# A two-block model on one core: attention masks on full rows, gate sigmoids at eviction, two modulation products moved, expert selection tied to the weight splits

## The chip, the core and the metric

One NeuronCore of a Trainium2 chip: TensorE (PE) for matmuls, VectorE (DVE), ScalarE (ACT), GpSimd (POOL) and the DMA queue of SyncE (SP). The metric is the device time of one execution in microseconds; a kernel is given by the median of its runs.

## The reference, cut to what matters

Two transformer-like blocks of width 1024 over 256 tokens, in float32. Block one mixes an mLSTM with four heads and an attention with eight heads of 64, gates the two with sigmoids, and ends in a gated feed-forward layer. With 256 tokens and blocks of 256 keys the attention is plain causal attention.

```python
mod = jnp.dot(c_act, ada_w[l]) + ada_b[l]
sh1, sc1, g1, sh2, sc2, g2 = jnp.split(mod, N_MOD, axis=-1)
h = modulate(rms_norm(x, norm1_g[l]), sh1, sc1)
z = jnp.einsum('bsd,de->bse', h, w_in[l]) + b_in[l]
...
ym = (hm.reshape(B, S, M_WIDTH) * jax.nn.sigmoid(mo)).astype(x.dtype)
ya = merge_heads(moba_attention(qa, ka, va))
merged = (jax.nn.sigmoid(ga) * jnp.einsum('bsm,md->bsd', ym, p_mlstm[l])
          + jax.nn.sigmoid(gb) * jnp.einsum('bsa,ad->bsd', ya, p_moba[l]))
x = x + g1[:, None, :] * jnp.einsum('bsd,de->bse', merged, w_out[l])
```

Block two has a pooling and a state-space mixer (SSD) with 16 heads and then chooses, for each token and each of eight heads, 16 of 16384 experts by product keys:

```python
seg = a_cs[..., :, None] - a_cs[..., None, :]
decay = jnp.exp(jnp.where(causal, seg, -jnp.inf))
...
v1, i1 = lax.top_k(s1, PEER_TOPK)
v2, i2 = lax.top_k(s2, PEER_TOPK)
top_s, pos = lax.top_k(cand, PEER_TOPK)
gates = jax.nn.softmax(top_s, axis=-1)
```

All 16384 experts are computed for all tokens as dense matmuls, and the gates choose among them afterwards.

## The kernel before

All weights stream through TensorE as slabs of 128 x 1024 (512 KB). A slab is loaded by SP (`raw`), copied by ScalarE into the rounded format fp32r (`hi`, L213), and the rest `lo = raw - hi` is formed by VectorE (L218) or GpSimd (L216). The activations are split in the same way, and each product is three matmuls (`mm3`, L273 to L276): 24 matmuls of 256 columns for a slab in `proj`. The order of the slabs is written out in the list `items` (L158 to L192); the modulation products ("ada", kind "d") lie between them: each loads 512 KB and is one VectorE multiplication with a sum (L230). `prep` works two slabs ahead (`LA = 2`); `hi` and `lo` have three buffers each, and a projection ends in one of three PSUM buffers `pp`. Other matmuls write to five buffers `sp`.

`cur["gp"]` says that every gp-th split goes to GpSimd; it is 2 from the eighth query slab to the 28th expert slab and otherwise 0. Side work is written as generators: `tick()` after a projection runs one step of the first one in `gens`.

The code states an order, and a planner in the framework chooses the final order on each engine by its own model of the times. `after(ins, prev)` (L89) fixes that `ins` stands behind `prev`; `act` fixes an activation behind its table load, and `table` a table load behind all activations of the table before.

Block one: the mLSTM (generator `mlstm`, L552), rotation of the query and key slabs (`rope`), value slabs, then 16 gate slabs (L717 to L722) whose results are evicted by ScalarE with a bias (L721), with `moba` (L659), the attention, as the generator beside them. `moba` makes the scores (L671, L672) in four groups of two banks: 128 queries against 256 keys, then 128 against 128; a mask of -1e30 is added by a matmul with an identity. After the 16 slabs come the sigmoid table, the mLSTM's output gate, one sigmoid over all of `sg`, and the merge (`pmo`, eight slabs, L740 to L751), then `wout`.

Block two: the decay masks of the 16 SSD heads (L926 to L933), made by a 48-row matmul and two mask matmuls for each head. The expert selection is the generator `topk` (L1083), four times: (head half, token half), about 16 steps each, beside 8 of the 16 query slabs and the 64 first expert slabs (`dblock`). The 64 next ones have `gstage` beside them, which builds the gate matrix.

Of the kernel before, what the change touches and what calls it, by code (L numbers as in the profile page):

```python
# [61 lines left out]
def two_block_kernel(ctx, tc, I, out, dbg=None):  # L62
# [120 lines left out]
    w_items("win", 28, ada_list(1, [2, 3, 4], "d"), 2)  # L183
    w_items("pmo", 8)
# [108 lines left out]
    gens = []  # L293

# [91 lines left out]
    with p1:  # L386
# [330 lines left out]
        for ab in range(2):  # L717
            for i in range(8):
                ps = pp()
                proj(ps)  # L720
                S.activation(sg[:, i, ab], ps[:, :T], AF.Identity, bias=pc("bga" if ab == 0 else "bgb", i))  # L721
                tick()  # L722
# [6 lines left out]
        for h in range(4):  # L729
            V.scalar_tensor_tensor(hm[:, h], hm[:, h], pc("mng", h), smo[:, h], OP.mult, OP.mult)  # L730
            S.activation(ymH[:, h], hm[:, h], AF.Copy)
            V.tensor_tensor(ymL[:, h], hm[:, h], ymH[:, h].bitcast(F32), OP.subtract)
        act(sg, sg, AF.Sigmoid)
# [99 lines left out]
    with ExitStack() as p3:  # L833
# [52 lines left out]
        identb = q3.tile([P, P], BF, name="identb")  # L886
        V.tensor_copy(identb, ident)
        trib = q3.tile([P, P], BF, name="trib")
        V.tensor_copy(trib, cs_("mB"))
# [32 lines left out]
        for i in (8, 9, 10, 11):  # L922
# [3 lines left out]
            for h in range(4 * i - 32, 4 * i - 28):  # L926
                ab = sp()
                se = id16[:, h:h + 1].to_broadcast([48, P])
# [145 lines left out]
    with ExitStack() as p4:  # L1074
# [8 lines left out]
        def topk(hq, tt):  # L1083
# [3 lines left out]
            for hf in range(2):  # L1087
# [8 lines left out]
                for h in range(4):  # L1096
                    V.max(v[:, h, 0:8], s_[:, h])
                    V.max_index(x[:, h, 0:8], v[:, h, 0:8], s_[:, h])
                    V.match_replace(s_[:, h], v[:, h, 0:8], s_[:, h], -3.0e38)
                    V.max(v[:, h, 8:16], s_[:, h])  # L1100
                    V.max_index(x[:, h, 8:16], v[:, h, 8:16], s_[:, h])
                    yield
# [5 lines left out]
            V.tensor_tensor(cand, vv[0].unsqueeze(3).to_broadcast([P, 4, 16, 16]),  # L1108
                            vv[1][:, :, None, :].to_broadcast([P, 4, 16, 16]), OP.add)
# [3 lines left out]
            for h in range(4):  # L1113
                ch = cand[:, h].rearrange("p a b -> p (a b)")
                V.max(ts_[:, h, 0:8], ch)
# [45 lines left out]
        for i in range(16):  # L1161
# [313 lines left out]
```

## Time and profile before

| | |
|---|---|
| median of the runs | 1427.33 us (1427.19 to 1429.57) |
| the profiled execution | 1433.29 us, span 1431.5 us |
| TensorE busy | 1389.7 us, 97% |
| VectorE busy | 1155.1 us, 81% |
| ScalarE busy | 708.8 us, 50% |
| GpSimd busy | 61.3 us, 4% |
| chain that ended last | PE 85%, DVE 10%, ACT 2%, DMA 2% |
| DMA | 285.92 MB, mean 200 GB/s |

A busy TensorE in the profile is one with a matmul in flight; since matmuls overlap, the count of matmuls in a stretch says more about its pace than its busy time. The granted clock is given as a share of 2.4 GHz. Two engines that stand for each other show up as idle time with the name of the instruction that ended it.

### The profile page before, as it was taken

The numbers are of one execution on the slowest core, as the hardware profiler recorded it, in microseconds if no ns is written. First come the engines' busy times: TensorE is split into PE (matmuls) and PEld (weight loads), VectorE is DVE, ScalarE is ACT, GpSimd is POOL, SyncE is SP. The second block draws the span as 40 slices with busy tenths as digits, with TensorE's granted clock in tenths as the row PEclk, the third lists the DMA queues.
The fourth block names the chain that finished last, engine by engine and source line by source line (L and its number), as shares of the span: only waits on it lengthen the run. The fifth ranks groups of instructions, "written<-read, shape, count | busy, mean of one in ns | idle before, by whom it ended". The sixth has DMA issues, their size and how long they took to land.

```text
span 1431.5 us, 28913 instructions
## 1 busy us (share of the span) xinstructions
PE 1389.7 (97%) x11842; PEld 1341.2 (94%) x11842; DVE 1155.1 (81%) x1995; ACT 708.8 (50%) x1052; POOL 61.3 (4%) x50
## 2 busy tenths in 40 slices
PE   8999989999999999998899999999999999999997
PEld 6888779899999788998899999999999999999997
DVE  7999558988888597789956978989689999675554
ACT  4555465554546846555554544444444443444443
POOL 0000000000000000123420000000000000000001
PEclk9999889999999999999999999999999999999999
DMA  9988416699995353554455555555655555676663
GB/s 319 341 289 314 148 47 192 229 350 343 330 317 207 104 155 125 163 161 149 162 188 181 177 166 174 163 165 172 180 164 161 177 161 172 200 215 213 208 205 103
DMA packets 78921, 285.92 MB, mean 200 GB/s; under 512 B 8786, under 2 KB 9186, under 8 KB 78660
## 3 DMA queue, kind: packets, MB, share of 16 engines
q1 hardware_dynamic: 78484, 282.60, 60.6%
q8 instruction: 93, 1.52, 0.4%
q0 software_dynamic: 304, 1.47, 0.3%
q14 instruction: 40, 0.33, 0.1%
HBM read 282.99 MB, written 1.05 MB: 198 GB/s over the span
## 4 chain that ended last, share of the span: by engine, by line
PE 85%; DVE 10%; ACT 2%; DMA 2%; issue 1%; SPq 0%; DVEq 0%; ACTq 0%
PE pp L274 17%; PE pp L276 17%; PE pp L275 17%; PE sp L1271 9%; PE sp L1274 8%; PE sp L1275 8%; DVE lo L218 3%; PE pp L1210 2%; ACT hi L213 1%; PE sp L671 1%; DMA raw<-in_wst 0%; DVE raw L230 0%; DMA ada<-in_wst 0%; DVE M L965 0%; PE sp L929 0%
## 5 line engine op out<-in xcount | busy, mean ns | idle before, releaser
L213 ACT ACTIVATE hi<-raw 128x1024 fp32r<-128x1024 f32 x382 | 404.6, 1060 | 562.7 <-PE pp L275 282.9
L218 DVE TENSOR_TENSOR lo<-raw,hi 128x1024 fp32r<-128x1024 f32 x364 | 450.3, 1238 | 141.3 <-ACT hi L213 140.5
L276 PE MATMUL pp<-nH,lo 128*128 128x256 f32 x1064 | 301.6, 285 | 16.1 <-DVE lo L218 16.1
L274 PE MATMUL pp<-nH,hi 128*128 128x256 f32 x1064 | 300.0, 283 | 1.5 <-ACT fs L107 0.9
L275 PE MATMUL pp<-nL,hi 128*128 128x256 f32 x1064 | 300.3, 283 | 0.0
L1271 PE MATMUL sp<-wHL,hi 128*128 128x256 f32 x992 | 279.5, 283 | 0.0
L1274 PE MATMUL sp<-wHL,hi 128*128 128x256 f32 x992 | 277.7, 281 | 0.0
L1275 PE MATMUL sp<-wHL,lo 128*128 128x256 f32 x992 | 273.8, 281 | 0.0
L274 PE MATMUL pp<-hH,hi 128*128 128x256 f32 (+1 forms) x824 | 237.0, 288 | 1.3 <-ACT sg L721 1.3
L276 PE MATMUL pp<-hH,lo 128*128 128x256 f32 (+1 forms) x824 | 234.6, 285 | 0.0
L275 PE MATMUL pp<-hL,hi 128*128 128x256 f32 (+1 forms) x824 | 233.6, 284 | 0.0
L276 PEld LDWEIGHTS pp<-nH,lo 128*128 128x128 f32 x1064 | 200.2, 189 | 19.4 <-DVE lo L218 19.3
L274 PEld LDWEIGHTS pp<-nH,hi 128*128 128x128 f32 x1064 | 200.7, 189 | 2.1 <-ACT fs L107 1.1
L275 PEld LDWEIGHTS pp<-nL,hi 128*128 128x128 f32 x1064 | 200.5, 189 | 0.1
L1271 PEld LDWEIGHTS sp<-wHL,hi 128*128 128x128 f32 x992 | 188.2, 190 | 0.0
L1274 PEld LDWEIGHTS sp<-wHL,hi 128*128 128x128 f32 x992 | 188.0, 189 | 0.0
L1275 PEld LDWEIGHTS sp<-wHL,lo 128*128 128x128 f32 x992 | 185.9, 190 | 0.0
L274 PEld LDWEIGHTS pp<-hH,hi 128*128 128x128 f32 x824 | 157.1, 191 | 2.7 <-ACT sg L721 1.5
L276 PEld LDWEIGHTS pp<-hH,lo 128*128 128x128 f32 x824 | 157.2, 191 | 1.1 <-issue 0.7
L275 PEld LDWEIGHTS pp<-hL,hi 128*128 128x128 f32 x824 | 157.3, 191 | 0.7 <-issue 0.5
L1214 DVE SCALAR_TENSOR_TENSOR W<-pp,W 128x512 f32<-128x512 f32 x64 | 86.1, 1346 | 22.3 <-PE pp L1210 22.3
L213 ACT ACTIVATE hi<-ada 128x1024 fp32r<-128x1024 f32 x52 | 55.1, 1059 | 67.3 <-PE pp L275 37.9
(442 smaller groups left out, 2146.9 us busy)
## 6 DMA issues: line engine op xcount, KB each, us to landing
raw<-in_edn SPq DMA_DIRECT2D x128, 512.0 KB, 3.6
raw<-in_eup SPq DMA_DIRECT2D x128, 512.0 KB, 4.2
raw<-in_ada SPq DMA_DIRECT2D x64, 512.0 KB, 5.0
raw<-in_win SPq DMA_DIRECT2D x34, 512.0 KB, 4.4
ada<-in_ada SPq DMA_DIRECT2D x32, 512.0 KB, 5.1
raw<-in_wgu SPq DMA_DIRECT2D x32, 512.0 KB, 4.5
ada<-in_win SPq DMA_DIRECT2D x18, 512.0 KB, 4.5
raw<-in_wdn SPq DMA_DIRECT2D x15, 512.0 KB, 5.8
```

Of the source, the lines that this page charges most:

```text
L213: S.activation(hi, raw, AF.Copy)
L218: cur["lo"] = V.tensor_tensor(lo, raw, hi.bitcast(F32), OP.subtract)
L274: m = PE.matmul(ps, lh, rh, start=start, stop=False)
L275: PE.matmul(ps, lh, rl, start=False, stop=False)
L276: PE.matmul(ps, ll, rh, start=False, stop=stop)
L671: PE.matmul(ps[:, j * T:j * T + ns], ro[rows, r, tt * P:(tt + 1) * P], ro[rows, 4 + r, :ns], start=True, stop=False)
L1210: PE.matmul(ps[:, t * 64:(t + 1) * 64], A[:, t].rearrange("p n d -> p (n d)"), B[:, j, t].rearrange("p n d -> p (n d)"), start=(j == 0), s ...
L1214: V.scalar_tensor_tensor(wv, ps.rearrange("p (t n) -> p t n", t=GT), 1.0 / GSC, wv, OP.mult, OP.mult)
L1271: m = PE.matmul(o, hi[:, b], wH, start=first, stop=False, skip_group_check=True)
L1274: PE.matmul(o, hi[:, b], wL, start=False, stop=False, skip_group_check=True)
L1275: return PE.matmul(o, lo[:, b], wH, start=False, stop=last, skip_group_check=True)
```

## The change

Five parts.

1. The list: the modulation products 2 and 3 of block one lie among slabs 11 to 27 of `win` in place of 2 to 27, and product 4 lies among the eight `pmo` slabs.
2. The masks: `moba` issues the score matmuls of two heads on opposite row halves in turn, into two banks, and adds both masks of a bank by one fp32r matmul on 128 rows. The SSD's `ArS` and `id16` are filled up with zeros to 128 rows, and its two mask matmuls become one.
3. The gates: from the tenth gate slab on, the eviction is the sigmoid itself; the table is loaded before it. The generator `gates` does the mLSTM's output gate and the first eight gates in pairs.
4. The merge: the split of a merged row moves into the loop over the rows.
5. The selection: most of the VectorE instructions of `topk`, and the first of each step of `gstage`, are fixed behind the VectorE split that was issued last; GpSimd takes every fourth split up to the 56th expert slab.

```diff
-    w_items("win", 28, ada_list(1, [2, 3, 4], "d"), 2)
-    w_items("pmo", 8)
+    w_items("win", 28, ada_list(1, [2, 3], "d"), 11)
+    w_items("pmo", 8, ada_list(1, [4], "d"))
...
+    def paced(ins):
+        after(ins, cur["lo"])
+        return ins
...
-        identb = q1.tile([P, P], BF, name="identb")
-        V.tensor_copy(identb, ident)
-        trib = q1.tile([P, P], BF, name="trib")
-        V.tensor_copy(trib, cs_("tri"))
+        identr = q1.tile([P, P], F32R, name="identr")
+        S.activation(identr, ident, AF.Copy)
+        trir = q1.tile([P, P], F32R, name="trir")
+        S.activation(trir, cs_("tri"), AF.Copy)
...
-                    ps = sp()
-                    rows = slice(64 * (c % 2), 64 * (c % 2) + 64)
-                    for j in range(2):
-                        r = 2 * (c // 2) + j
-                        PE.matmul(ps[:, j * T:j * T + ns], ro[rows, r, tt * P:(tt + 1) * P], ro[rows, 4 + r, :ns], start=True, stop=False)
-                        PE.matmul(ps[:, j * T + tt * P:j * T + ns], identb, trib, start=False, stop=True)
+                    if c % 2 == 0:
+                        pair = [sp(), sp()]
+                        for j in range(2):
+                            r = 2 * (c // 2) + j
+                            for i, ps in enumerate(pair):
+                                rows = slice(64 * i, 64 * i + 64)
+                                PE.matmul(ps[:, j * T:j * T + ns], ro[rows, r, tt * P:(tt + 1) * P], ro[rows, 4 + r, :ns],
+                                          start=j == 0, stop=False, skip_group_check=True)
+                        for ps in pair:
+                            PE.matmul(ps.rearrange("p (g s) -> p g s", g=2)[:, :, tt * P:ns], identr,
+                                      trir[:, None, :].to_broadcast([P, 2, P]), start=False, stop=True, skip_group_check=True)
+                    ps = pair[c % 2]
...
-        drain_gens()
-        table("sigmoid_and_others")
-        act(smo, smo, AF.Sigmoid)
-        ada_run()
...
-        act(sg, sg, AF.Sigmoid)
+        def gates(n):
+            for h in range(4):
+                act(smo[:, h], smo[:, h], AF.Sigmoid)
+                V.scalar_tensor_tensor(hm[:, h], hm[:, h], pc("mng", h), smo[:, h], OP.mult, OP.mult)
+                S.activation(ymH[:, h], hm[:, h], AF.Copy)
+                V.tensor_tensor(ymL[:, h], hm[:, h], ymH[:, h].bitcast(F32), OP.subtract)
+                if h % 2:
+                    yield
+            for i in range(0, n, 2):
+                v = sg[:, i:i + 2, 0]
+                act(v, v, AF.Sigmoid)
+                yield
+
+        direct = False
+        for n in range(16):
+            ab, i = n // 8, n % 8
+            if n == 9:
+                table("sigmoid_and_others")
+                direct = True
+                gens.append(gates(8))
+            ps = pp()
+            proj(ps)
+            if direct:
+                act(sg[:, i, ab], ps[:, :T], AF.Sigmoid, bias=pc("bgb", i))
+            else:
+                S.activation(sg[:, i, ab], ps[:, :T], AF.Identity, bias=pc("bga" if ab == 0 else "bgb", i))
+            tick()
+        drain_gens()
+        act(sg[:, 0, 1], sg[:, 0, 1], AF.Sigmoid)
+        ada_run()
...
             V.tensor_tensor(sg[:, e, 0], sg[:, e, 0], sg[:, e, 1], OP.add)
-        for e in range(8):
             S.activation(mgH[:, e], sg[:, e, 0], AF.Copy)
...
-        ArS = q3.tile([48, 384], F32R, name="ArS")
-        id16 = q3.tile([48, 16], F32R, name="id16")
+        ArS = q3.tile([P, 384], F32R, name="ArS")
+        id16 = q3.tile([P, 16], F32R, name="id16")
+        G.memset(ArS.bitcast(F32), 0.0)
+        G.memset(id16.bitcast(F32), 0.0)
...
-                PE.matmul(ab[:, :P], identb, trib, start=False, stop=False, skip_group_check=True)
-                PE.matmul(ab[:, T:384], identb, trib, start=False, stop=True, skip_group_check=True)
+                PE.matmul(ab.rearrange("p (g s) -> p g s", g=2)[:, :, :P], identr, trir[:, None, :].to_broadcast([P, 2, P]),
+                          start=False, stop=True, skip_group_check=True)
...
-                    V.max(v[:, h, 0:8], s_[:, h])
-                    V.max_index(x[:, h, 0:8], v[:, h, 0:8], s_[:, h])
+                    paced(V.max(v[:, h, 0:8], s_[:, h]))
+                    paced(V.max_index(x[:, h, 0:8], v[:, h, 0:8], s_[:, h]))
...
-                cur["gp"] = 2
+                cur["gp"] = 4
...
-            cur["gp"] = 2 if n2 < 28 else 0
+            cur["gp"] = 4 if n2 < 56 else 0
```

## Rows read from the trace of the kernel before

**Rows 1.** Busy us by stretch: PE, PEld, DVE, ACT, POOL; clock, DMA share, GB/s.
```profile
80.00:107.00 27.00, 26.74 (x167) 23.48 (x167) 27.00 (x49) 12.34 (x19) 0.00 (x0) 1.00 0.81 296
107.00:161.80 54.80, 53.36 (x393) 47.83 (x392) 47.41 (x72) 29.06 (x45) 0.00 (x0) 1.00 0.81 284
161.80:190.40 28.60, 27.49 (x122) 19.96 (x121) 15.65 (x43) 17.54 (x47) 0.00 (x0) 0.70 0.13 42
190.40:232.00 41.60, 38.61 (x277) 34.73 (x277) 22.54 (x38) 19.21 (x32) 0.00 (x0) 0.96 0.38 124
220.00:230.00 10.00, 10.00 (x86) 10.00 (x85) 9.06 (x16) 4.52 (x7) 0.00 (x0) 1.00 0.61 189
```

**Rows 2.** The same view: the selection's stretch, and one of the gate matrix.
```profile
610.00:730.00 120.00, 108.07 (x896) 106.45 (x895) 113.28 (x359) 60.78 (x89) 44.36 (x17) 1.00 0.49 160
1100.00:1200.00 100.00, 100.00 (x1070) 99.14 (x1070) 99.66 (x136) 41.00 (x40) 0.00 (x0) 1.00 0.53 165
```

**Rows 3.** Timeline of PE, attention scores: start, us, engine, line, operation, tiles, shapes.
```profile
161.76 0.70 PE L671 MATMUL sp<-ro 64*128 64x256 f32 x2
162.55 0.70 PE L671 MATMUL sp<-ro 64*128 64x256 f32 x2
...
168.74 0.79 PE L671 MATMUL sp<-ro 64*128 64x128 f32 x2
169.69 0.79 PE L671 MATMUL sp<-ro 64*128 64x128 f32 x2
```

**Rows 4.** Timeline of PE, output of two SSD heads and the matmuls after it.
```profile
516.21 0.65 PE L947 MATMUL sp<-M,xtok 128*64 128x256 f32 x4
516.69 0.39 PE L950 MATMUL sp<-M,xtok 128*64 128x128 f32 x4
```

**Rows 5.** Busy time by stretch, two slices of 2.5 us.
```profile
180.00:182.50 2.50, 2.50 (x14) 2.50 (x14) 0.87 (x4) 2.48 (x11) 0.00 (x0) 0.50 0.02 7
212.50:215.00 2.50, 2.50 (x14) 2.50 (x14) 2.50 (x6) 0.42 (x1) 0.00 (x0) 0.54 0.70 226
```

**Rows 6.** PE by line, 161.7 to 184 us: xcount | busy us, mean ns | idle before.
```profile
L276 PE MATMUL pp<-hH,lo 128*128 128x256 f32 x12 | 5.1, 428 | 0.0
```

**Rows 7.** Timeline of ACT, the sigmoid over all gates.
```profile
188.81 3.63 ACT L107 ACTIVATE sg<-sg 128x4096 f32<-128x4096 f32 x1
```

**Rows 8.** Waits of PE, 186 to 232 us: us in total, times, longest.
```profile
PE pp L274 <- ACT ymH L731: 1.5, 1, 1.5
```

**Rows 9.** ACT by line, 107 to 162 us.
```profile
L721 ACT ACTIVATE sg<-pp,prm 128x256 f32<-128x256 f32 x13 | 6.0, 458 | 0.0
```

**Rows 10.** DVE by line, 80 to 107 us: modulation products.
```profile
L230 DVE SCALAR_TENSOR_TENSOR raw<-raw,crow 128x1024 f32<-128x1024 f32 x5 | 6.0, 1206 | 0.0
```

**Rows 11.** Part 5 of the page: copies of the slabs.
```profile
L213 ACT ACTIVATE hi<-raw 128x1024 fp32r<-128x1024 f32 x382 | 404.6, 1060 | 562.7 <-PE pp L275 282.9
```

**Rows 12.** Timeline of PE, two decay masks one after the other.
```profile
473.47 0.44 PE L929 MATMUL sp<-ArS,id 48*128 48x384 f32 x1
...
474.06 0.44 PE L929 MATMUL sp<-ArS,id 48*128 48x384 f32 x1
```

**Rows 13.** Busy time by stretch: the decay masks.
```profile
461.00:500.00 39.00, 37.97 (x275) 32.11 (x274) 23.21 (x48) 30.12 (x70) 0.00 (x0) 1.00 0.35 109
```

**Rows 14.** Waits of PE, 610 to 730 us.
```profile
PE pp L276 <- DVE lo L218: 11.9, 8, 2.4
```

**Rows 15.** Timelines of POOL, DVE and PE around one wait.
```profile
678.37 2.39 POOL L216 TENSOR_TENSOR lo<-raw,hi 128x1024 fp32r<-128x1024 f32 x1 [2.64 <-ACT hi L213]
...
678.58 3.26 DVE L218 TENSOR_TENSOR lo<-raw,hi 128x1024 fp32r<-128x1024 f32 x1
...
681.90 0.39 PE L276 MATMUL pp<-nH,lo 128*128 128x256 f32 x1 [1.27 <-DVE lo L218]
```

**Rows 16.** DVE by line, 610 to 735 us, and POOL, 600 to 735 us: splits.
```profile
L218 DVE TENSOR_TENSOR lo<-raw,hi 128x1024 fp32r<-128x1024 f32 x21 | 31.9, 1521 | 7.2 <-ACT hi L213 7.2
...
L216 POOL TENSOR_TENSOR lo<-raw,hi 128x1024 fp32r<-128x1024 f32 x18 | 46.8, 2598 | 79.2 <-ACT hi L213 63.9 <-DVE x L1098 5.1 <-PE pp L275 4.1
```

More of the change, by code (lines that the diff above doesn't have):

```diff
@@ L716, in two_block_kernel @@
         sg = q1.tile([P, 8, 2, T], F32, name="sg")
[L717 to L722, printed above, removed]
-        drain_gens()
-        table("sigmoid_and_others")
-        act(smo, smo, AF.Sigmoid)
-        ada_run()
         ymH = q1.tile([P, 4, T], F32R, name="ymH", tag="vm")
         ymL = q1.tile([P, 4, T], F32R, name="ymL", tag="E")
[L729 to L732, printed above, removed]
-        act(sg, sg, AF.Sigmoid)
+        def gates(n):
[27 more added lines that the diff above has]
+        ada_run()
         mgH = q1.tile([P, 8, T], F32R, name="mgH", tag="rin")
@@ L881, in two_block_kernel @@
         cbT = q3.tile([P, 2, 384], F32, name="cbT")
-        ArS = q3.tile([48, 384], F32R, name="ArS")
-        id16 = q3.tile([48, 16], F32R, name="id16")
+        ArS = q3.tile([P, 384], F32R, name="ArS")
+        id16 = q3.tile([P, 16], F32R, name="id16")
+        G.memset(ArS.bitcast(F32), 0.0)
+        G.memset(id16.bitcast(F32), 0.0)
         S.activation(id16[0:32], ident[0:32, 0:16], AF.Copy)
         S.activation(id16[32:48], ident[0:16, 0:16], AF.Copy)
[L886 to L889, printed above, removed]
+        identr = q3.tile([P, P], F32R, name="identr")
+        S.activation(identr, ident, AF.Copy)
+        trir = q3.tile([P, P], F32R, name="trir")
+        S.activation(trir, cs_("mB"), AF.Copy)
         yv = q3.tile([P, 8, T], F32, name="yv")
@@ L927, in two_block_kernel @@
                 ab = sp()
-                se = id16[:, h:h + 1].to_broadcast([48, P])
+                se = id16[:, h:h + 1].to_broadcast([P, P])
                 PE.matmul(ab[:, :384], se, ArS, start=True, stop=False, skip_group_check=True)
-                PE.matmul(ab[:, :P], identb, trib, start=False, stop=False, skip_group_check=True)
-                PE.matmul(ab[:, T:384], identb, trib, start=False, stop=True, skip_group_check=True)
+                PE.matmul(ab.rearrange("p (g s) -> p g s", g=2)[:, :, :P], identr, trir[:, None, :].to_broadcast([P, 2, P]),
+                          start=False, stop=True, skip_group_check=True)
                 act(M[:, h, :T], ab[:, :T], AF.Exp, bias=cols[:, 1, 0, h:h + 1])
@@ L1107, in topk @@
             cand = w4.tile([P, 4, 16, 16], F32, name="cand")
-            V.tensor_tensor(cand, vv[0].unsqueeze(3).to_broadcast([P, 4, 16, 16]),
-                            vv[1][:, :, None, :].to_broadcast([P, 4, 16, 16]), OP.add)
+            paced(V.tensor_tensor(cand, vv[0].unsqueeze(3).to_broadcast([P, 4, 16, 16]),
+                            vv[1][:, :, None, :].to_broadcast([P, 4, 16, 16]), OP.add))
             yield
@@ L1114, in topk @@
                 ch = cand[:, h].rearrange("p a b -> p (a b)")
-                V.max(ts_[:, h, 0:8], ch)
+                paced(V.max(ts_[:, h, 0:8], ch))
                 V.max_index(po[:, h, 0:8], ts_[:, h, 0:8], ch)
@@ L1124, in topk @@
                 if hf == 0:
-                    V.tensor_scalar(ju, pof, 4, None, op0=OP.logical_shift_right)
+                    paced(V.tensor_scalar(ju, pof, 4, None, op0=OP.logical_shift_right))
                 else:
-                    V.tensor_scalar(ju, pof, 15, None, op0=OP.bitwise_and)
+                    paced(V.tensor_scalar(ju, pof, 15, None, op0=OP.bitwise_and))
                 jf = w4.tile([P, 64, 2], F16, name="jf")
@@ L1137, in topk @@
             ga_ = gat[tt][:, hs]
-            V.tensor_tensor(ga_, ts_, ts_[:, :, 0:1].to_broadcast([P, 4, 16]), OP.subtract)
+            paced(V.tensor_tensor(ga_, ts_, ts_[:, :, 0:1].to_broadcast([P, 4, 16]), OP.subtract))
             act(ga_, ga_, AF.Exp)
@@ L1197, in gstage @@
             A = q5.tile([P, GT, 64, 2], F16, name="A")
-            V.tensor_tensor(A, iob.rearrange("p (n d) -> p n d", d=2)[:, None].to_broadcast([P, GT, 64, 2]),
-                            i1d[:, tsl, None, :].to_broadcast([P, GT, 64, 2]), OP.is_equal)
+            paced(V.tensor_tensor(A, iob.rearrange("p (n d) -> p n d", d=2)[:, None].to_broadcast([P, GT, 64, 2]),
+                                  i1d[:, tsl, None, :].to_broadcast([P, GT, 64, 2]), OP.is_equal))
             yield
```

8 lines of the change are left out of this document (4 added, 4 removed).

## The prediction

> **What bounds the kernel now.** I read the page first: TensorE is busy 97% of the span and heads 85% of the chain that ended last. So the time is TensorE's, and a change pays only where TensorE stands, runs at the lower clock, or does work it could do faster. I then cut the span into stretches and looked for the few that are not dense. Three stand out. First the attention stage: between 161.8 and 190.4 us the granted clock averages 0.70 and only 122 matmuls run; in the 41.6 us after that, 277; a dense stretch handles 86 in 10 us [rows 1]. Second a shorter stretch around the decay masks of block two. Third the expert selection, where TensorE is busy 108 of 120 us while the vector engine is busy 113 [rows 2]. Elsewhere the vector engine is busy 99.7 of 100 us and TensorE still never waits [rows 2]: a full vector queue by itself does no harm. 10 us / 86 gives 0.116 us from one 256-column projection matmul to the next, and 24 of them, one weight slab, 2.8 us.
>
> **The change part by part.** All sums go against the profiled execution's own 1433.29 us (span 1431.5); the median of the runs shown is 1427.33, 6 us less, and I carry the same difference in us over to it.
>
> *Scores of the attention.* Before, each of 16 head-and-half scores is two passes on 64 rows, then a bf16 mask on 128 rows. Start to start this is 0.79 us per head at full clock for 256 keys (8 heads), 0.95 us at half clock for 128 keys (8 heads) [rows 3]: 6.3 + 7.6 = 13.9 us. The change issues two heads of opposite row halves in turn and adds both masks of a bank in one matmul on 128 rows. The unknown is whether opposite halves run at once. The nearest row is the second block's output matmul, where two heads write opposite column halves: its four passes of 256 columns are through 0.48 us after their start [rows 4]. So, with halves at once, a group of four heads costs 2 x 0.48 + two masks of 0.116 + about 0.2 for switching, 1.4 us with 256 keys, and 0.95 us with 128: two groups each, 4.7 us. One after the other it is 2.3 and 1.4, so 7.4 us. I take 4.7, since that row is a concurrent one: **-9.2** (-6.5 at the other end). On this the Trainium skill (TensorE: Matmul & The Clock Gate, Part 3: Packing small matmuls — row/col tiling) says that matmuls on different row strips of the array run at once; by it the sum is the 4.7, and no run here shows it yet for row strips.
>
> *Clock.* TensorE falls to 0.50 (1.2 GHz) in the midst of these 64-row scores, and is still there when projections alone run [rows 5]. 36 projection matmuls ran between the first score and its return to 2.4 GHz (three lines of 12, one shown) [rows 6], each 0.1 us longer than at 2.4 GHz: 3.6 us. If the scores are short and lie on both row halves there is no reason to fall: **-3.5**, or 0 if it falls all the same.
>
> *Gate sigmoids.* Before, ScalarE loads the sigmoid table only after all scores, and one 3.63 us activation over all gates stands ahead of small copies that TensorE waits for [rows 7]. TensorE stands 1.1 + 3.0 = 4.1 us in the two stretches from 161.8 us on [rows 1], longest 1.5 us for a `ymH` copy [rows 8], and the clock dips behind them to 0.54 in a stretch that handles 14 matmuls for a dense 21.5 [rows 5], 0.9 us more. With sigmoids spread over evictions and five small generator steps these go: **-5**, at worst -2. The ScalarE work itself is unchanged: an eviction costs 0.46 us [rows 9], and I take the same for a sigmoid.
>
> *What the sigmoid at eviction adds.* The table load waits for the last exponential of the attention, and evictions 10 to 16 of the gates now stand behind it on ScalarE. Before, 13 gate evictions ran before the scores [rows 9]: they fed TensorE while the chain of block one's first mixer finished. Now 9 plus the 3 that fit in the `pp` buffers can. Behind the waiting eviction stand the next `hi` copies on ScalarE; TensorE waits for them and for `pp`. If the scores move forward as below, this costs nothing; if they start when they did, one slab of 2.8 us is missing and the chain to the last exponential (4 groups) lies bare, up to 9. I take **+2** (0 to +9).
>
> *Modulation products.* 24 of them ran among slabs 2 to 27, at 1.21 us each on the vector engine [rows 10]; seven fall in 80 to 107 us (five in the row, two on the other buffer), where that engine is busy 27.00 of 27 us [rows 1]. Sixteen now run among slabs 11 to 27, eight behind the merge slabs, with their eight 512 KB loads, which SP issues in list order between the merge weights. The early stretch is freed of 8.5 us, the scores can come some 8 us sooner, and what TensorE stands between 80 and 161.8 us, 0.3 + 1.4 [rows 1], goes: **-1.5** (0 to -1.7). The merge stage gets worse: it now keeps the vector engine busy 9.06 us in the 10 us of 3.6 slabs [rows 1], 2.5 per slab; with 1.28 more it wants 3.8 against 2.8 on TensorE, so +8 us over eight slabs. Splits are made two slabs ahead, 5.6 us less a copy of 1.06 [rows 11] and a split of 1.2, so 3.3 us of this is covered, and attention outputs that still lie among the merge cover the rest. I take **+2.5** (0 to +5). The loads would want two 512 KB slabs per 2.8 us, 374 GB/s, where the fullest row here has 296 [rows 1]; at 3.8 us it is 276, so they hide behind the vector engine, and at 296 they alone would cost 8 x 0.7, the same upper end.
>
> *Merge in pieces.* The split of the merged rows moves into the loop. TensorE is dense in the last merge slabs [rows 1], so 0: the splits already run under the next slabs' matmuls. Without that cover each pair, 256 of a slab's 1024 columns, would cost some 0.6 us of a slab's 1.06 + 1.21, eight of them 5.
>
> *Decay masks.* A head costs 0.59 us from start to start [rows 12]: a 48-row matmul of 384 columns and two bf16 masks. On 128 rows, at 0.116 us for 256 columns, 384 + 256 columns cost 0.29. At 0.3 saved, less where other work lies between (bf16 masks then overlap it), sixteen give up to -4.7; I count on 0.2 each, -3.3. ScalarE is busy 30 of 39 us here [rows 13], so it can follow most of this: **-2.7** (-1 to -4.7). The two extra GpSimd fills of `ArS` and `id16` fall where that queue is idle; bf16 copies become ScalarE copies of 0.3 us: 0.
>
> *Expert selection.* TensorE waits eight times for `lo`, 11.9 us in all [rows 14]. Each wait has the same look: a GpSimd split runs 2.39 us, the vector engine's own split, started beside it, takes 3.26 instead of 1.21 us, and TensorE stands 1.27 us at its end [rows 15]. Over the stretch 21 splits average 1.52 us and 18 GpSimd ones 2.60 [rows 16]. Selection work is bunched: three of the four groups (16 steps each, token half by head half) lie in this stretch. The vector engine spent 113 less 32 for splits, 81 us, on them [rows 2, 16], 27 per group, 108 for four. Spread over 72 slabs (201 us) with 56 splits of 1.21 us this is 176 of 201, 88%. The GpSimd splits stay 16 but come every fourth slab. So waits should nearly vanish; the prize is 12, and I leave 1 for the tails of the groups, whose steps are longest: **-11** (-6 to -12).
>
> Against it speaks the Trainium skill (SBUF — State Buffer, Who interferes with whom): the port pair that VectorE shares with GpSimd is locked for a whole instruction, and a vector instruction with two SBUF inputs waits out a GpSimd one that reads SBUF. The row of the 3.26 us split [rows 15] agrees; by it all 16 remaining splits may each cost the vector engine their full length.
>
> Sum: -9.2 - 3.5 - 5 + 2 - 1.5 + 2.5 - 2.7 - 11 = **-28.4**: 1404.9 profiled, 1399 for the median.
>
> **The rivals** (medians).
> 1. *The scores don't gain what they should*: halves run one after the other (+2.7) and the clock falls as before (+3.5). For it: no row shows row halves at once. 1405.
> 2. *Sigmoids hold the evictions* for the full 9: the gates' `pp` buffers fill and TensorE stands before the table load. For it: 13 against 12; against it: the freed vector engine. 1406.
> 3. *The vector engine takes over*: merge +5 and selection only -6, because GpSimd's lock stays. If each of the 16 costs it 2.6 us, it wants up to 42 + 108 + 68 = 218 us of the 201. 1406.
> 4. *Pacing makes it slower.* Each selection step now stands behind the split of the slab two ahead, and that split waits until TensorE gives back a `hi` buffer. Once the lead of 3.3 us is used up, a slab takes copy 1.06 + split 1.21 + step 108/70 = 1.5, 3.8 us in place of 2.8. On 30 of 72 slabs this eats all that the rest brings (+30 against -28); on 45 it gives +45 and, less the 28 that the sum brings, +17, 1444. Against it: the stretch with 99.7 of 100 us busy and no wait [rows 2].
> 5. *The scheduler undoes the pacing* by moving selection in bunches anyway, since only some of its instructions are tied: selection 0, 1410.
>
> **How the numbers follow.** Forecast 0.50 (its own range 1391 to 1404); rivals 1, 2 and 3 or pairs of them 0.28; rival 5 0.07; rival 4 0.08; between 1416 and 1430 0.04, of which half within 0.2% of before; still better than 1391 0.03. A measurement of this kernel can tell about 0.2%, 3 us. The range 1389 to 1416 keeps about 0.85. Faster 0.89, same 0.03, slower 0.08. The likeliest is 1399.
>
> **What the profile after would show.** Scores: eight mask matmuls of 256 columns; start to start 1.4 us for four heads; clock 1.00 through the stage. If the clock column again has 0.50, step two was wrong. Gates: no 3.63 us activation, a table load in the midst of the gate evictions, and no long `pp` wait ahead of it. Merge: waits for `lo` there mean the +2.5 was too small. Decay masks: 0.3 us from head to head, ScalarE above 85%. Selection: `lo` waits under 3 us in all and the vector engine near 90% but nowhere 100% for long. I would be wrong above all if the instruction order, which the planner sets anew, puts the scores later or the selection in bunches.

## The result, and the profile after

The changed kernel takes **1405.74 us** (median of 4 executions, 1405.11 to 1405.84) where the kernel before took 1428.45 beside it (1427.19 to 1433.03): ratio 0.9834, interval 0.9811 to 0.9858, 22.7 us less. A second set gave 1406.31 against 1429.36, ratio 0.9833 (0.9814 to 0.9853), 23.1 less. The forecast was 1399, 28.4 less. The measured time lies inside its wide range (1389 to 1416), but 6.7 us above the forecast, outside the forecast's own range (1391 to 1404) and where rivals 1 to 3 had put it (1405, 1406, 1406). So the number alone does not bear the forecast out; the traces have to tell. The profiled execution took 1405.74 us, its own median, where the sum of the prediction, made against the profiled execution before, had come to 1404.9.

Busy time by stretch, columns as in [rows 1]. First the stretches that answer to [rows 1] (up to the scores, scores and gates, merge, output projection), then the two of [rows 2]:

```profile
80.00:107.00 27.00, 27.00 (x170) 24.89 (x170) 24.38 (x41) 14.10 (x23) 0.00 (x0) 0.94 0.65 213
107.00:145.70 38.70, 38.70 (x275) 33.64 (x274) 33.41 (x50) 20.00 (x30) 0.00 (x0) 1.00 0.73 253
145.70:172.50 26.80, 24.37 (x183) 21.56 (x182) 21.65 (x55) 21.43 (x61) 0.00 (x0) 1.00 0.44 145
172.50:205.70 33.20, 30.51 (x234) 28.02 (x233) 25.90 (x46) 16.29 (x30) 0.00 (x0) 0.95 0.77 271
205.70:217.00 11.30, 11.30 (x98) 11.30 (x97) 8.35 (x15) 4.49 (x7) 0.00 (x0) 1.00 0.73 224
...
600.00:720.00 120.00, 120.00 (x1014) 120.00 (x1013) 103.42 (x320) 64.95 (x97) 24.22 (x10) 1.00 0.59 180
```

The scores begin at 145.8 us instead of 161.8, and where the granted clock was 0.70 it is 1.00. TensorE still stands 2.4 us there and 2.7 in the merge. In the selection it is busy 120 of 120 us (108 before), with the vector engine at 103 instead of 113: no wait for `lo` is left of the eight in [rows 14].

The scores on TensorE, to hold against [rows 3]: four heads of 256 keys, their two masks, and, 7.5 us later, two heads of 128 keys with their mask:

```profile
145.76 1.14 PE L677 MATMUL sp<-ro 64*128 64x256 f32 x8
146.82 0.51 PE L680 MATMUL sp<-trir,identr 128*128 128x256 f32 x2
147.26 0.49 PE L677 MATMUL sp<-ro 64*128 64x256 f32 x2
...
153.24 0.71 PE L677 MATMUL sp<-ro 64*128 64x128 f32 x4 [0.73 <-ACT P L107]
153.88 0.39 PE L680 MATMUL sp<-trir,identr 128*128 128x256 f32 x1
```

A group of four with 256 keys takes 1.50 us from start to start (147.26 - 145.76). The groups with 128 keys were pulled apart by the planner into two heads of one row half each, 0.86 us a piece (0.64 to the mask, 0.22 for it). In all 2 x 1.50 + 4 x 0.86 = 6.4 us against 13.9.

The gates: the table load and the first sigmoid at eviction (ScalarE), and TensorE behind them:

```profile
162.34 1.28 ACT L94 ACT_TABLE_LOAD   x1
163.63 0.84 ACT L107 ACTIVATE sg<-pp,prm 128x256 f32<-128x256 f32 x2
```
```profile
164.16 0.39 PE L274 MATMUL pp<-hH,hi 128*128 128x256 f32 x1 [1.70 <-ACT sg L107]
```

The merge, waits of TensorE from 172 to 206 us, and the clock behind them (two slices) and at the start of the feed-forward stage:

```profile
PE pp L274 <- DVE sg L773: 1.9, 1, 1.9
PE pp L276 <- DVE lo L218: 0.6, 1, 0.6
```
```profile
195.00:197.50 2.50, 1.89 (x10) 1.72 (x11) 2.50 (x4) 0.42 (x1) 0.00 (x0) 0.82 0.20 46
197.50:200.00 2.50, 2.50 (x14) 2.50 (x13) 2.50 (x6) 0.75 (x2) 0.00 (x0) 0.50 0.94 349
272.50:275.00 2.50, 2.50 (x13) 2.50 (x13) 2.50 (x5) 0.00 (x0) 0.00 (x0) 0.50 1.06 416
```

The vector engine's product into `sg` is late, TensorE stands 2.5 us in two waits, and the clock falls to 1.2 GHz: 14 matmuls in 2.5 us where 21.5 fit. A fall of this kind, a few us long, is called a spell below. The trace has five of them ahead of its last 5 us, at 80, 197, 272, 487 and 542 us. One costs about 1.7 us: the two slices here, at 0.82 and 0.50, lose 0.45 + 1.25.

The decay masks on TensorE, against [rows 12], the stretch of [rows 13] and its densest part, and the waits from 452 to 552 us:

```profile
459.10 0.34 PE L956 MATMUL sp<-ArS,id 128*128 128x384 f32 x1
459.28 0.28 PE L957 MATMUL sp<-trir,identr 128*128 128x256 f32 x1
459.39 0.34 PE L956 MATMUL sp<-ArS,id 128*128 128x384 f32 x1
```
```profile
442.00:482.00 40.00, 39.23 (x316) 38.53 (x315) 28.54 (x56) 33.56 (x80) 0.00 (x0) 1.00 0.43 133
465.00:480.00 15.00, 15.00 (x126) 15.00 (x125) 9.05 (x15) 14.98 (x39) 0.00 (x0) 1.00 0.39 116
```
```profile
PE pp L276 <- DVE lo L218: 2.7, 2, 2.2
```

0.29 us from head to head instead of 0.59; ScalarE is now full, and the wait behind the masks has grown from 1.5 to 2.2 us.

**Where the time went, by stages.** ScalarE copies the weight slabs in one fixed order, so the start of the same copy in two traces tells how far one kernel is ahead. From the copy timelines of each kernel, in us: *attention* is from the first input slab to the first output slab, *middle* on to the second block's first input slab, *block two* on to the first query slab, *selection* on to the first gate-matrix slab.

| kernel | attention | middle | block two | selection | median, range |
|---|---|---|---|---|---|
| before | 158.9 | 217.4 | 141.6 | 452.2 | 1428.45, 1427.2-1433.0 |
| before again | 156.0 | 215.8 | 143.7 | 452.1 | 1430.26, 1429.3-1431.2 |
| after | 144.4 | 218.1 | 139.5 | 441.1 | 1405.74, 1405.1-1405.8 |
| after again | 145.0 | 218.0 | 140.2 | 441.0 | 1406.31, 1404.7-1407.9 |
| old scores | 152.2 | 215.8 | 137.7 | 441.0 | 1409.72, 1408.1-1411.4 |
| serial halves | 145.0 | 217.4 | 139.8 | 441.1 | 1405.42, 1401.1-1408.9 |
| old sigmoids | 143.9 | 217.5 | 136.9 | 441.0 | 1400.94, 1399.7-1402.2 |
| old products | 147.9 | 215.7 | 137.3 | 441.1 | 1406.63, 1404.9-1408.0 |
| no pacing | 143.3 | 215.8 | 140.1 | 448.2 | 1411.71, 1408.7-1413.2 |
| old share | 145.2 | 215.7 | 140.4 | 440.0 | 1402.90, 1400.9-1405.0 |
| no GpSimd | 142.6 | 215.8 | 139.6 | 440.3 | 1406.09, 1401.7-1413.1 |
| old decay masks | 141.8 | 215.7 | 140.6 | 441.0 | 1404.10, 1402.1-1407.1 |
| merge free | 152.4 | 215.7 | 133.7 | 440.1 | 1404.82, 1404.6-1410.2 |
| merge free, new sigmoids | 144.9 | 220.4 | 140.4 | 440.2 | 1406.63, 1405.4-1408.0 |

The stages are those of one profiled execution each (for the first row the one of 1433.29 us, which is not among the four of its median), so the scatter has to be known first. Six of these kernels (after, after again, no pacing, old share, no GpSimd, old decay masks) issue the same attention: 141.8 to 145.2, mean 143.7. Selection repeats within 0.1. Medians scatter by several us. The runs also came in sets, and the kernel before beside them had a median of 1432.32 us (before again, old scores, serial halves, old sigmoids), 1429.36 (after again, old products, no pacing, old share) and 1431.60 (no GpSimd, old decay masks and the two with the merge free), so medians of different sets compare to some 3 us only. Terms below 3 us are therefore read from the stages.

### The profile page after: what moved, and what is told of

Its sections match the earlier page's. It is cut to its first block, busy times and chain, and to the rows that moved or that the text cites. A ratio compares the mean times of both kernels' runs of the same rounds, so it can differ in the third digit from the quotient of the medians.

```text
span 1404.0 us, 28893 instructions
## 1 busy us (share of the span) xinstructions
PE 1369.6 (98%) x11818; PEld 1333.8 (95%) x11818; DVE 1155.2 (82%) x1993; ACT 707.4 (50%) x1063; POOL 53.5 (4%) x50
## 4 chain that ended last, share of the span: by engine, by line
PE 60%; DVE 1%; issue 0%; ACT 0%; DVEq 0%; ACTq 0%
PE pp L274 10%; PE pp L276 10%; PE pp L275 10%; PE sp L1298 9%; PE sp L1302 9%; PE sp L1301 9%; PE pp L1237 2%; PE sp L1119 1%; DVE lo L218 0%; PE sp L1342 0%; DVE A L1225 0%; ACT hi L213 0%; DVEq L1488 0%; DVE xT L1350 0%; DVE B L1229 0%
## 5 line engine op out<-in xcount | busy, mean ns | idle before, releaser
L1302 PE MATMUL sp<-wHL,lo 128*128 128x256 f32 x992 | 276.7, 281 | 0.0
```

What stands on the lines that cost most here:

```text
L1302: return PE.matmul(o, lo[:, b], wH, start=False, stop=last, skip_group_check=True)
```

## The experiments

Each is the kernel after with one edit, if nothing else is said.

**The kernel before again, and the kernel after again.** No edit.

> The kernel before, unchanged, once more. Its profiled execution took 1433.29 us, its other executions 1427.2 to 1429.6; the prediction carried those 6 us over to the changed kernel, whose profiled execution and median agree (1405.74). Theory: the 6 us are the kernel's own, time that only some of its executions lose in stretches that the change makes dense, so they go with the change. Then a new profile of a shorter execution is near 1428 and differs from the first in the stretches with a lower clock or with waits, and nowhere else. Rival: recording a profile costs this kernel 6 us. Then the new profile is 1433 again and every execution without one is 1427 to 1430.

> The changed kernel, unchanged, once more, on the chip of the next three. Its first four executions agree within 0.7 us (1405.1 to 1405.8), while one-part variants of it spread by 2.5 to 8 us from one execution to the next, and in their traces the short spells at 1.2 GHz (some 3.5 us each, 1.7 us lost) stand in other places from run to run. Theory: whether the clock falls behind a wait is open in each execution, and the first four agree by accident; then the spells stand elsewhere here and the times spread from 1402 to 1408. Rival: this kernel's waits fix the spells, the same five places as in the first trace, and the times lie within 1 us of 1405.7.

The new profiled execution of before took 1431.23 us, others of that kernel up to 1433.7: it is not the recording that costs 6 us, the rival fell. The theory held half: the slower stretch at 212.5 us in [rows 5] is gone in the new trace,

```profile
212.50:215.00 2.50, 2.50 (x24) 2.50 (x23) 2.50 (x6) 1.06 (x1) 0.00 (x0) 1.00 0.82 256
```

but another spell has come at 478 us, in a stretch that the change does not make dense. After again shows the five spells of the first trace within 2 us of their places, as the rival has it, and a sixth, in the score stage:

```profile
157.50:160.00 2.50, 2.50 (x14) 2.50 (x14) 1.50 (x6) 2.50 (x11) 0.00 (x0) 0.51 0.28 67
```

Its times spread from 1404.7 to 1407.9: the close agreement of the first four executions was chance. The times go, for the most part, with the granted clock: of the seven executions of before beside after again, those with a mean clock of 0.988 took 1432.1 and 1432.5 us, those with 0.991 1428.1 and 1429.0 (in another set it is less clean, 1430.8 at 0.988 and 1433.0 at 0.990).

**Old scores.**
```
-  pair of banks, heads of opposite row halves in turn, one fp32r mask of 256 columns per bank
+  one head after the other, two bf16 masks of 128 columns per bank
```


> The changed kernel with the attention scores as before: one head after the other, two bf16 masks of 128 columns per bank. The scores in the trace after take 6.4 us where 13.9 was read before. Theory: the scores come back at 13.9 and the clock falls in their midst as before, 7.5 + 3.5 = +11: 1417 us, with 0.50 in the clock column behind them. Rival one: the clock had fallen before because TensorE waited and ran thin in that stage, not because of the 64-row matmuls: +7.5, 1413, clock 1.00. Rival two: what waits for the scores is late anyway (the sigmoid evictions that now stand behind the last exponential), so a longer chain also lengthens the 1.7 us wait there: +14, 1420.

Attention 152.2, +8.5 on the mean. The median is 4 us higher, and only 2 by its ratio to the kernel before beside it (0.9847 against 0.9834); the middle and block two, which the edit does not touch, are 4.1 us shorter in this trace than in the one after. The clock falls again in the midst of the scores:

```profile
155.00:157.50 2.50, 2.50 (x7) 1.21 (x6) 0.85 (x3) 1.64 (x8) 0.00 (x0) 0.50 0.27 108
```

Before it fell, TensorE had waited for nothing and handled 17 and 11 matmuls in the two slices of 2.5 us up to 152.5 us and 8 in the one in which it fell; so rival one's +7.5 is near in size but wrong in its reason, and the theory's +11 is 2.5 too much. The whole attention stage, here and then in the kernel after:

```profile
62.70:215.00 152.30, 149.26 (x1012) 131.79 (x1011) 121.52 (x215) 89.90 (x177) 0.00 (x0) 0.93 0.62 213
```
```profile
61.30:205.70 144.40, 139.28 (x1004) 126.10 (x1003) 120.37 (x216) 89.15 (x177) 0.00 (x0) 0.98 0.66 226
```

A mean clock of 0.93 over 152.3 us is some 10 us lost, 0.98 over 144.4 some 3 (0.96 to 0.99 in the six kernels). So up to 7 of the 8.5 us come back through the clock, an estimate that holds where TensorE had work at the time, and the longer score matmuls by themselves return little. The longer chain did not add to a wait (rival two): the wait for the first sigmoid is not there any more, and the merge waits 2.2 us instead of 1.9.

**Serial halves.**
```
-  for j in range(2):
-      for i, ps in enumerate(pair):
+  for i, ps in enumerate(pair):
+      for j in range(2):
```


> The changed kernel with one edit: in a pair of score banks both heads of one row half are issued first, then both of the other, so that neighbouring matmuls lie on the same rows; masks unchanged. Only the two groups with 256 keys keep the paired order in the kernel after, with starts 7 ns apart on opposite halves and 0.21 us from pair to pair. Theory: opposite halves run at once, so four more steps of 0.21 us per group, +0.84 twice: 1407.4 us, a group of four heads 2.3 us instead of 1.50. Rival one: the array takes them one after the other whatever the order, and the equal starts are how the trace counts: 1405.7, same. Rival two: 64 rows at a time lower the clock: +1.7 and +3.5, 1411.

Median 1405.42, attention 145.0, and the group takes the same time:

```profile
146.71 1.14 PE L677 MATMUL sp<-ro 64*128 64x256 f32 x8
147.78 0.51 PE L680 MATMUL sp<-trir,identr 128*128 128x256 f32 x2
148.21 1.14 PE L677 MATMUL sp<-ro 64*128 64x256 f32 x8
```

The theory fell, and rival one with it, though it had the time right: eight passes take 1.14 us, where before two passes of one head took 0.70 [rows 3]. Two halves do run at once, and over these four matmuls the order in which they are issued does not matter. What counts is that both halves are there: the 128-key groups, two heads of one half alone, go one pass after the other.

**Old sigmoids.**
```
-  sigmoid at eviction from the tenth gate on; the earlier gates and the mixer's in pieces
+  sixteen copies, table load, one activation over all gates
```


> The changed kernel with the gate sigmoids as before: all 16 gate evictions copy, then the table is loaded, then one activation over all gates; products, masks, merge and pacing stay as changed. Theory of the prediction: the gates' sigmoids in pieces gave 5 us and the wait at the first sigmoid eviction took 2 back (1.7 in the trace after), so undoing them gives +3: 1408.7 us, with a 3.6 us activation and TensorE waiting for the small copies behind it. Rival: the merge is now held by the vector engine (waits for sg and lo of 1.9 to 0.6 us and a clock dip behind them), and what is late before it costs nothing more: 0, or -1.7 as the wait at the eviction goes, 1404 to 1406.

Median 1400.94, the lowest of all: ratio to before 0.9785 (0.9771 to 0.9800), below the interval of after. But not through the attention, which takes 143.9 (mean 143.7): the rival held. At the first merge slab this kernel is 3.7 us ahead of after, and it loses 3.3 us of that in the merge, where TensorE waits five times, 3.7 us in all (2.5 in the kernel after), and the clock stays down longer (0.57, 0.50 and 0.56 in the three slices from 192.5 us):

```profile
179.55 3.63 ACT L107 ACTIVATE sg<-sg 128x4096 f32<-128x4096 f32 x1
183.09 0.36 ACT L721 ACTIVATE ya<-sp 128x256 fp32r<-128x256 f32 x1
```
```profile
PE pp L274 <- DVE sg L757: 1.1, 1, 1.1
PE pp L275 <- DVE ya L722: 0.9, 1, 0.9
...
PE pp L274 <- ACT ya L721: 0.5, 1, 0.5
```

Its lead comes later, in the middle and block two, which the edit does not touch; in its trace the spells at 272 and 540 us that the trace after has are missing, though one at 452 us has come. Why its executions are all shorter is open; the kernel after was not run beside them.

**Old products.**
```
-  w_items("win", 28, ada_list(1, [2, 3], "d"), 11)
-  w_items("pmo", 8, ada_list(1, [4], "d"))
+  w_items("win", 28, ada_list(1, [2, 3, 4], "d"), 2)
+  w_items("pmo", 8)
```


> The changed kernel with the modulation products as before: all 24 from the third input slab on, none in the merge. At the end of the merge the changed kernel is 15.1 us ahead; the scores as before take 9.3 of it back and the sigmoids as before nothing (-0.4), so 5 to 6 us belong to the products, or to nothing that was tried. Theory: the products are those 5 to 6: with them early the vector engine holds the scores back again and the evictions wait behind the last exponential, +5.5, 1411, though the merge no longer waits for sg and lo. Rival one (by the prediction's sum, early -1.5 and merge +2.5): the merge's waits of 1.9 + 0.6 us and the clock spell behind them go and 1.5 comes back early, -1 to -3, 1403 to 1405. Rival two: scores 8 us later cost the evictions the full 9 less what the merge gives back: +7, 1413.

Attention 147.9: +4.2, near the theory; the median hides it (+0.3 on after again, which ran beside it). The scores start 11 us later than in after, stand closer together, and the clock falls among them, new form or not. Over the stage its mean is 0.95 against 0.98, some 4 us more lost, so here too the clock can be most of the effect:

```profile
156.77 1.13 PE L677 MATMUL sp<-ro 64*128 64x256 f32 x8
...
161.39 0.71 PE L677 MATMUL sp<-ro 64*128 64x128 f32 x4 [0.61 <-ACT P L107]
...
164.09 1.22 PE L677 MATMUL sp<-ro 64*128 64x128 f32 x4
```
```profile
162.50:165.00 2.50, 2.50 (x9) 2.05 (x9) 1.22 (x5) 2.50 (x15) 0.00 (x0) 0.50 0.00 0
```

**No pacing, and the old GpSimd share.**
```
 def paced(ins):
-    after(ins, cur["lo"])
     return ins
```
```
-  cur["gp"] = 4 ... cur["gp"] = 4 if n2 < 56 else 0
+  cur["gp"] = 2 ... cur["gp"] = 2 if n2 < 28 else 0
```


> The changed kernel without the ties of selection steps to the last weight split; the GpSimd share stays at every fourth slab up to the 56th. From the start of the expert stage to its end the changed kernel gains 11.0 us on the one before (16.5 ahead at the query stage, 27.6 at the gate matrix). Theory: the ties carry it; without them the steps stand in bunches again and TensorE waits for lo: +8 to +11, 1414 to 1417, 8 to 10 us of waits for lo between 600 and 740 us. Rival: the smaller number of GpSimd splits per slab carries it, because each of them stretches the vector engine's split beside it: 0 to +2, 1406 to 1408.

> The changed kernel with the GpSimd share as before: every second slab up to the 28th instead of every fourth up to the 56th (16 to 18 splits either way); the ties stay. Theory: the ties carry the gain and the share is worth little, because the splits only move: 0 to +1, 1405 to 1407. Rival: the GpSimd split's 2.4 us and the vector split stretched from 1.2 to 3.3 us beside it make the waits, and at every second slab they come twice as often: +4 to +8, 1410 to 1414, with waits for lo of over 1 us in the first 28 slabs.

Selection 448.2 without the ties (+7.1) and 440.0 with the old share (-1.1). With the ties undone the vector splits are stretched again, up to 3.37 us, and TensorE waits (7.1 us is a little under the theory's 8 to 11):

```profile
L218 DVE TENSOR_TENSOR lo<-raw,hi x75: 1202/1219/3371, 601.7 to 879.4; 128x1024 fp32r<-128x1024 f32 x75
...
  PE pp L276: 5.9, 6
```

The same view of the kernel after (least, median and longest split in ns), without any such wait:

```profile
L218 DVE TENSOR_TENSOR lo<-raw,hi x78: 1198/1224/1230, 600.3 to 879.2; 128x1024 fp32r<-128x1024 f32 x78
```

So the ties carry it, and the timelines show at least one way. One GpSimd split and what the vector engine did in that time, first without the ties, then in the kernel after:

```profile
639.29 2.40 POOL L216 TENSOR_TENSOR lo<-raw,hi 128x1024 fp32r<-128x1024 f32 x1 [8.59 <-ACT hi L213]
639.39 3.37 DVE L218 TENSOR_TENSOR lo<-raw,hi 128x1024 fp32r<-128x1024 f32 x1
```
```profile
771.07 2.41 POOL L216 TENSOR_TENSOR lo<-raw,hi 128x1024 fp32r<-128x1024 f32 x1 [9.95 <-ACT hi L213]
771.76 1.77 DVE L1131 CAST xf<-x 128x64 f16<-128x64 uint32 x1
773.86 1.23 DVE L218 TENSOR_TENSOR lo<-raw,hi 128x1024 fp32r<-128x1024 f32 x1 [0.33 <-ACT hi L213]
```

In the kernel after none of the 91 vector splits between 580 and 900 us overlaps one of the 16 GpSimd splits; the steps of the selection stand beside those instead. In the kernel before 9 of 82 overlap one, and five of these take 1.8 to 3.3 us; with the ties and the old share three do, and one of them takes 1.66. Ties and old share give 452.2 - 440.0 = 12.2, new share alone 4.0, both 11.1: beside the ties the new share takes 1.1 back.

**No GpSimd splits in the selection.**
```
-  cur["gp"] = 4 ... cur["gp"] = 4 if n2 < 56 else 0
+  cur["gp"] = 0 ... cur["gp"] = 0
```


> The changed kernel without GpSimd splits in the expert stage: all splits there run on the vector engine, ties kept. Theory by the prediction's sum: 14 to 16 more splits of 1.22 us raise the vector engine from 88 to 96 us in 100, so waits for lo come back: +2 to +5, 1408 to 1411. Rival: a GpSimd split costs the vector engine, in the selection steps beside it, about what it saves: 0 to -2, 1404 to 1406, and the vector engine's selection steps get shorter.

Selection 440.3, no wait for `lo`: the rival held. Whether the ties are still needed without GpSimd splits was not run. The median (1406.09) says nothing, with executions from 1401.7 to 1413.1. From 610 to 880 us the splits on the vector engine take 17.0 us more (92.7 to 109.7), but all its busy time grows by only 9.3 (235.3 to 244.6), since short steps are no longer held up; the two that shrink most, in the kernel after, and then here:

```profile
L1131 DVE CAST xf<-x 128x64 f16<-128x64 uint32 x7 | 4.1, 584 | 0.1
L1154 DVE TENSOR_SCALAR ju<-po 128x64 uint32<-128x64 uint32 x4 | 3.0, 741 | 0.0
```
```profile
L1131 DVE CAST xf<-x 128x64 f16<-128x64 uint32 x7 | 1.3, 186 | 0.1
L1154 DVE TENSOR_SCALAR ju<-po 128x64 uint32<-128x64 uint32 x4 | 0.8, 188 | 0.0
```

The Trainium skill (SBUF — State Buffer, Who interferes with whom), which the prediction set against the change, says that a GpSimd instruction locks the shared port pair for its whole length. The stretched splits of [rows 15] and of no pacing agree, and so do the short steps. The kernel after cannot speak against it with its splits (1.23 us at most), since none of them ran beside a GpSimd split.

**Old decay masks.**
```
-  ArS, id16 on 128 rows; one fp32r mask matmul of 256 columns per head
+  ArS, id16 on 48 rows; two bf16 mask matmuls of 128 columns per head
```


> The changed kernel with the decay masks of block two as before: 48-row matmuls and two bf16 masks per head. From the second block's first input slab to the query stage the changed kernel takes 139.5 us in its first trace, the one before 141.6. Theory of the prediction: 0.2 to 0.3 us per head on TensorE, so undoing costs +2.7 (1 to 4.7): 1408 to 1409. Rival: ScalarE, busy all of the 20 us in the midst of this stage in the trace after, sets its end, and the 2.2 us wait for lo that now stands behind the masks takes back what the matmuls give; then undoing costs 0 to +0.8, 1405.7 to 1406.5, and that wait is shorter.

Block two takes 140.6, where nine kernels with the new masks (the two combinations below left out) took 136.9 to 140.4, mean 139.1: +1.5. The wait behind the masks is 1.5 us again, as before, so 0.7 of the gain goes into it; that ScalarE, full there, is the cause is argued. Between theory and rival; the spells in this stage (one of 1.7 us here, two in after) are as large as the effect, and with 1.7 us taken off for each it is 138.9 against 136.1 in after, near the 2.7 of the theory. Done for all traces, which supposes that TensorE had work throughout, this gives 133.5 to 136.8 for the nine with the new masks and 138.2 and 138.6 for the two of before: the theory's side. The median (1404.10) cannot decide it.

**Two combinations.** Products all in the input slabs, old share; the first with old sigmoids, the second with new ones.
```
+  w_items("win", 28, ada_list(1, [2, 3, 4], "d"), 8)
+  w_items("pmo", 8)
```


> A combination: the changed kernel with the sigmoids as before, all 24 modulation products between the 9th and the last input slab and none in the merge, and the old GpSimd share. Theory: with eight products in its midst the merge is held by the vector engine, which hides the 3.7 us that the old sigmoids gain up to its start; without them these are kept, TensorE no longer waits for sg and lo there (1.9 + 0.6 us), and the share gives 1.1: 1396 to 1400. Rival: 24 products among the input slabs hold the scores back as the old products did (4 us late at the merge's start): 1403 to 1406.

> The same combination, but with the sigmoids as changed (from the tenth gate on at eviction, the rest in pieces). Theory: the sigmoids at eviction cost 3 to 4 us up to the merge (wait of 1.7 to 2.2 us at the first of them, fewer gates to cover the score chain) and only a merge held by the vector engine hid that: 3 to 4 us more than the other combination, 1400 to 1403. Rival: once the merge is free, the one large activation and the small copies behind it are what TensorE waits for, and the pieces gain the 3 us of the prediction: 1395 to 1397, 3 us less than the other combination.

Both theories fell; the first one's rival, that products among the input slabs hold the scores back, had its time right (1404.82 in 1403 to 1406). With the products back there and the old sigmoids the attention takes 152.4: the scores begin at 159.9 us, and TensorE waits for their chain:

```profile
PE sp L719 <- ACT PT L712: 5.9, 1, 5.9
PE sp L709 <- DVE P L700: 2.9, 1, 2.9
```

That the gates which could have covered the chain are used up by then is argued from the order, not shown by itself. With the new sigmoids the attention takes 144.9. Here that edit is worth 7.5 us in the attention, as the second one's rival has it in direction, though the median is 1.8 higher; in the kernel after it is worth nothing. Neither combination beats old sigmoids (1400.94), which beats both kernels. (The first gains 6 us back in block two, which neither edit touches; the planner orders that stage anew in each kernel, and which difference does it is open.)

## Why the prediction was right or wrong

*Direction and places: right.* Faster, and the traces give attention and selection as the two places, with no gain in the middle.

*From the sum to the median: the step that failed.* I carried the 6 us between the profiled execution before and its median over to the changed kernel. They were not a fixed cost of being recorded, and the changed kernel does not have them. They were how that one execution fell out, and the changed kernel's fell out otherwise. The 1427.33 that I mapped to was low besides: beside the later sets the kernel before had medians of 1429.36 to 1432.32. Profile to profile the gain is 27.5 (23.7 in the second pair), median to median 22.7 and 23.1. The sum should have been set against the spread of the runs.

*Scores and clock, -9.2 - 3.5: too large, and wrongly shared out.* Four heads of 256 keys cost 1.50 us (forecast 1.4), and the row halves do run at once, as the Trainium skill says (TensorE: Matmul & The Clock Gate, Part 3: Packing small matmuls — row/col tiling): the trace agrees, eight passes in 1.14 us for two in 0.70. But I took the pairing for granted where the planner issues the matmuls; the 128-key groups came out unpaired, 3.4 us for 1.9. Undone as a whole the scores return 8.5 of 12.7, and up to 7 of that through the clock, which I had priced at 3.5. The clock's fall was laid to the 64-row form alone; old products shows it with the new form, when the scores stand close together behind late work, and after again has a spell in that stage too.

*Gate sigmoids, -5 + 2: too large by 3.* The wait at the first sigmoid was 1.7, near the forecast 2. The stalls that were to go are real in the kernel before [rows 7, 8], and yet in the changed kernel the edit is worth 0.2: what the old sigmoids are ahead at the start of the merge, 3.7 us, they lose in it but for 0.4.

*Modulation products, -1.5 + 2.5: wrong sign.* They gained 4.2. The merge has the waits that were forecast (2.5 us and a spell of 1.7), but from its first slab on it is only 0.5 longer with the products than without (33.1 and 32.6 us). The early term was the error: I priced only what TensorE stood between 80 and 161.8 us, and not that the scores come 11 us sooner. That gates and projections are then left to stand between them and cover their chain is argued; shown are the wider spacing and the higher clock.

These three terms lean on the same cover. Undone one by one they return 8.5, 0.2 and 4.2, together 12.9 of the 13.7 between the means of before and after, and the sum of the prediction for the stage was 14.7: right as a sum, with each part wrong, so the agreement is in part luck. One execution for each, with a scatter of up to 1.9 us about the mean, lies under these figures.

*Merge in pieces, 0:* not tried by itself; no row speaks against it.

*Decay masks, -2.7:* 0.29 us per head as forecast; 1.5 by the stages as they stand and 2 to 5 with the spells taken off, with ScalarE full as foreseen and a wait 0.7 longer.

*Expert selection, -11: right,* 11.1 by the stage, with no wait for `lo` left. The stretched split of [rows 15] was the right thing to look at: in the kernel after no vector split runs beside a GpSimd split. Its parts were not right: the ties with the old share gave 12.2, and the GpSimd share that I counted as a help costs 1.1.

*The rivals.* Rivals 1 to 3 had the time but not the way: the row halves run at once, the wait at the first sigmoid was 1.7 us and not 9, and the selection gave its 11. Rival 3 showed in the merge, and was paid for by the earlier scores. Rivals 4 and 5 did not come: the split never got late behind a selection step.

## What to carry to other kernels

Price a step that is moved by what it lets start earlier, not only by the idle time it leaves; and where several edits shorten or cover one exposed chain, sum the chain once, since each edit's worth depends on the others (here 0.2 or 7.5 us for the same one). Filler work on a busy in-order queue pays when it is tied to the stream that it must not delay. Before a profiled time is mapped to a median, look at how far executions of the same kernel lie apart.

## What the runs showed of the hardware

The granted clock fell to 1.2 GHz for a few us behind waits of TensorE of 1 to 3 us, and also where TensorE had not stood at all (in old scores, and at 80 us in the trace after, with no wait since 60 us); each such spell cost about 1.7 us. It differs between executions of one kernel (at 212 us in the first trace of before and not in the second). At 272 us it fell in both traces of after, where the longest wait for `lo` just ahead was 1.2 and 1.4 us, and in neither of no pacing and old share, where the same wait was 0.6 us. The four executions of one kernel lay 0.7 to 11.4 us apart, more than most parts of this change are worth. Matmuls of 64 rows on opposite halves overlapped also when two of one half were issued first. Of the nine vector splits that overlapped a GpSimd split in the trace before, the three that had begun ahead of it took 1.20 us, and five of the six that began during it 1.8 to 3.3.
